# Down projection of a decoder layer: weight sums by adding DMAs, products reordered, a longer tile-by-tile end

## The chip, the cores and the metric

The kernel runs on one NeuronCore of a Trainium2 chip. Its time is in microseconds of the device, as the median of several runs. The profile is that of one more execution with the hardware profiler on. Times inside a profile are counted from the start of its span.

## The reference, cut to what matters

The kernel computes one whole decoder layer on a sequence of 1024 tokens with 1024 channels, in float32. The change touches only its last part, the down projection of the gated MLP, the norm of its output, and the residual sum:

```python
def conv_glu_ffn(h, w_up, conv_w, conv_b, w_down):
    u = causal_dwconv(h @ w_up, conv_w) + conv_b
    a, b = jnp.split(u, 2, axis=-1)
    return (jax.nn.silu(a) * b) @ w_down
...
        y = conv_glu_ffn(rmsnorm(h, g[4]), ffn_w_up[l], ffn_conv_w[l], ffn_conv_b[l], ffn_w_down[l])
        h = h + rmsnorm(y, g[5])
```

The hidden width is 2816, so the down projection is a product of 1024 x 2816 by 2816 x 1024.

## The kernel before

**The product.** The down projection is done by Strassen's scheme with seven products, M1 to M7, in place of eight block products. Rows (tokens), columns and the inner dimension are each halved. The 22 blocks of 128 hidden channels are taken in 11 pairs, the k pairs (`kp`): the first block of a pair belongs to the first half of the inner dimension, the second to the second. For each product and k pair, `down_operands` builds an operand tile `w` of the tag "w" (4 buffers), which holds a left block A (hidden channels by 512 tokens) and a right block B (hidden channels by 512 output columns), each in two float32r parts, high and low: ScalarE copies the high part, VectorE subtracts it from the float32 value to make the low part. `mm3` then multiplies high by high, high by low and low by high. A k pair is 12 matmuls of 128x128 by 128x512: four token tiles q, three each.

**The sums.** Most products need a sum or difference of two A blocks, of two B blocks or of both. A blocks are loaded once from `mid_d` in HBM, where the up projection left them, and stay in tiles named `ma`. B blocks are loaded anew for each use, from the weights, into tiles `rb` (tags "raw" and "braw", 2 buffers each, used in turn). A sum of A blocks is made by GpSimd (line 1299); one of B blocks by GpSimd as well, or by VectorE where the product also has a sum of A blocks (line 1301). Both go to tiles of the tag "sum" (`sM` in the profile). The split of a tile with two sums is `split` (lines 132 and 133); that of other tiles is lines 1308 to 1313.

**The order.** `todo` lists the steps (product, k pair) in order, M4, M3, M5, M2, M1, M6, M7, and `fetch(4)` keeps four operand tiles prepared or being prepared. A list scheduler of the framework then sets each engine's instruction order. The four accumulators of a product are PSUM banks; M6 adds onto the banks of M2 and M7 onto those of M1. When a token tile of a product is finished, `done` adds it from PSUM into the float32 tiles `yacc` (VectorE), and where a half row of the output is complete, `square` (ScalarE) sums its squares and `gained` (VectorE) multiplies it by the norm's gain. `final` makes the root factor, adds `yacc` times the factor to the residual `fin`, and stores the result. For token tiles 4 to 7 the finals are put off into a list `pend` and taken from it during M7, one at each odd k pair. The last four k pairs (`LAST`) of M7 are done token tile by token tile, with `final` behind each. The residual tiles `fin` have two buffers.

Of the kernel before, what the change touches and what calls it, by code (L numbers as in the profile page):

```python
# [7 lines left out]
F32 = mybir.dt.float32  # L8
F32R = mybir.dt.float32r
I32 = mybir.dt.int32  # L10
AF = mybir.ActivationFunctionType
ALU = mybir.AluOpType
# [4 lines left out]
P = 128  # L17
T = 1024
D = 1024
# [50 lines left out]
def hybrid_layer(  # L70
# [4 lines left out]
    nc = tc.nc  # L75
    act, dve, pe, sync = nc.scalar, nc.vector, nc.tensor, nc.sync

    def pool(name, bufs=1, side=None, space=None):
        kw = {} if space is DRAM else {"reuse_waits": "tile"}
        if side is not None:  # L80
            kw["side"] = side
        if space is not None:
            kw["space"] = space
        return tc.tile_pool(name=name, bufs=bufs, **kw)
# [16 lines left out]
    mid_d = dram.tile([NFF, P, T], F32, name="mid_d")  # L101

    const = ctx.enter_context(pool("const"))
    wpool = ctx.enter_context(pool("wpool"))
# [13 lines left out]
    def psum(tag, name):  # L118
        p, tags = psum_pool[0]
        return p.tile([P, 512], F32, tag=tag, name=name, bufs=tags[tag])  # L120
# [9 lines left out]
    def split(w, raw, gain=None):  # L130
        if gain is None:
            act.activation(w[:, 0], raw, AF.Copy)  # L132
            dve.tensor_tensor(w[:, 1], raw, w[:, 0], op=ALU.subtract)  # L133
        else:
            act.activation(w[:, 0], raw, AF.Identity, scale=gain)
            dve.scalar_tensor_tensor(out=w[:, 1], in0=raw, scalar=gain, in1=w[:, 0],
                                     op0=ALU.mult, op1=ALU.subtract)

    def raw_tile(shape, name):
        return wpool.tile(list(shape), F32, tag="raw", name=f"raw_{name}", bufs=2)  # L140
# [99 lines left out]
    HS = (slice(0, 512), slice(512, 1024))  # L240
# [299 lines left out]
    pend = []  # L540
# [487 lines left out]
    for t in range(NC):  # L1028
# [20 lines left out]
        r = rms_r(ss, 1, "r2")  # L1049
# [197 lines left out]
    for j in range(PLAIN, NFF):  # L1247
        if j + 1 < NFF:
# [7 lines left out]

    dr = ctx.enter_context(pool("dr", side="right"))
    dl = ctx.enter_context(pool("dl"))  # L1260
    g5 = row_gain(5, gbp)
    NP = NFF // 2
    yacc = [dl.tile([P, D], F32, name=f"yacc{t}") for t in range(NC)]
    ss5 = small(NC * 2, "ss5", bufs=1)
    LAST = 4

    PRODS = (("M4", ("22",), ("21", "11", -1)), ("M3", ("11",), ("12", "22", -1)),
             ("M5", ("11", "12", 1), ("22",)), ("M2", ("21", "22", 1), ("11",)),
             ("M1", ("11", "22", 1), ("11", "22", 1)), ("M6", ("21", "11", -1), ("11", "12", 1)),
             ("M7", ("12", "22", -1), ("21", "22", 1)))  # L1270
    res = {}

    def a_block(b, kp):

        if (b, kp) not in res:
            res[b, kp] = (dr if b == "22" and kp < 8 else dl).tile([P, 512], F32, name=f"ma{b}_{kp}")
            sync.dma_start(out=res[b, kp], in_=mid_d[2 * kp + int(b[1]) - 1][:, HS[int(b[0]) - 1]])
        return res[b, kp]

    n_step = [0]  # L1280

    def down_operands(m, kp):
        name, ab, bb = PRODS[m]
        p, tag = ((wpool, "raw"), (dr, "braw"))[n_step[0] % 2]
        n_step[0] += 1
        A_s = [a_block(b, kp) for b in ab[:2]]
        rb = p.tile([P, 2, 512], F32, tag=tag, name=f"rb{name}_{kp}", bufs=2)

        at = lambda b: w_down[2 * kp + int(b[0]) - 1][:, HS[int(b[1]) - 1]]
        bs = bb[:2]  # L1290
        for i, b in enumerate(bs):
            sync.dma_start(out=rb[:, i], in_=at(b))
        w = wpool.tile([P, 2, 2, 512], F32R, tag="w", name=f"w{name}_{kp}", bufs=4)
        sums = None
        if len(ab) == 3 or len(bb) == 3:
            sums = dr.tile([P, 2, 512], F32, tag="sum", name=f"s{name}_{kp}", bufs=2)
        alu = lambda s: ALU.add if s > 0 else ALU.subtract
        if len(ab) == 3:
            nc.gpsimd.tensor_tensor(sums[:, 0], A_s[0], A_s[1], op=alu(ab[2]))  # L1299
        if len(bb) == 3:  # L1300
            (dve if len(ab) == 3 else nc.gpsimd).tensor_tensor(sums[:, 1], rb[:, 0], rb[:, 1], op=alu(bb[2]))
        if len(ab) == 3 and len(bb) == 3:

            split(w, sums)
        else:
            for i, r in enumerate((sums[:, 0] if len(ab) == 3 else A_s[0], sums[:, 1] if len(bb) == 3 else rb[:, 0])):
                if name == "M2" and i == 1:
                    act.activation(w[:, 0, i], r, AF.Copy, scale=-1.0)
                    dve.scalar_tensor_tensor(out=w[:, 1, i], in0=r, scalar=-1.0, in1=w[:, 0, i],
                                             op0=ALU.mult, op1=ALU.subtract)  # L1310
                else:
                    act.activation(w[:, 0, i], r, AF.Copy)
                    dve.tensor_tensor(w[:, 1, i], r, w[:, 0, i], op=ALU.subtract)
        return w

    def square(t, n):
        jk = dl.tile([P, 512], F32, tag="junk", name="sqj", bufs=2)
        act.activation(jk, yacc[t][:, HS[n]], AF.Square, accum_out=ss5[:, 2 * t + n:2 * t + n + 1])

    def add_to(t, n, o, sign=1):  # L1320
        y = yacc[t][:, HS[n]]
        dve.tensor_tensor(y, y, o, op=ALU.add if sign > 0 else ALU.subtract)

    def gained(t, n):
        y = yacc[t][:, HS[n]]
        dve.tensor_tensor(y, y, g5[:, HS[n]], op=ALU.mult)

    def final(t, fin, first):

        r = sqrt_r(ss5_sum(t), 1, "r5")  # L1330
        for i, n in enumerate((first, 1 - first)):
            dve.scalar_tensor_tensor(out=fin[:, HS[n]], in0=yacc[t][:, HS[n]], scalar=r, in1=fin[:, HS[n]],
                                     op0=ALU.mult, op1=ALU.add)
            (sync, nc.scalar)[i].dma_start(out=out[t * P:(t + 1) * P, HS[n]], in_=fin[:, HS[n]])
# [3 lines left out]
        dve.tensor_tensor(s1, ss5[:, 2 * t:2 * t + 1], ss5[:, 2 * t + 1:2 * t + 2], op=ALU.add)  # L1338
        return s1

    def residual(t):
        fin = dl.tile([P, D], F32, tag="fin", name=f"fin{t}", bufs=2)
        sync.dma_start(out=fin, in_=h2_d[t])
        return fin

    def done(name, q, o):

        lo, hi = q, q + 4
        if name == "M4":
            act.activation(yacc[hi][:, HS[0]], o, AF.Copy)  # L1350
            act.activation(yacc[lo][:, HS[0]], o, AF.Copy)
        elif name == "M3":
            act.activation(yacc[lo][:, HS[1]], o, AF.Copy)
            act.activation(yacc[hi][:, HS[1]], o, AF.Copy)
        elif name == "M5":
            add_to(lo, 0, o, -1)
            add_to(lo, 1, o)
            square(lo, 1)
            gained(lo, 1)
        elif name == "M2":  # L1360
            add_to(hi, 0, o, -1)
            square(hi, 0)
            gained(hi, 0)
        elif name == "M1":
            add_to(hi, 1, o)
        elif name == "M6":
            add_to(hi, 1, o)
            square(hi, 1)
            gained(hi, 1)
            pend.append(lambda: final(hi, residual(hi), 0))  # L1370
        else:
            add_to(lo, 0, o)
            square(lo, 0)
            gained(lo, 0)
            final(lo, fins.pop(lo), 1)

    fins = {}
    todo = [(m, kp) for m in range(len(PRODS)) for kp in range(NP)]
    dops = {}

    def fetch(n):
        while todo and len(dops) < n:
            s = todo.pop(0)
            dops[s] = down_operands(*s)

    def step_mm(o, w, q, start, stop, onto):
        s = slice(q * P, (q + 1) * P)
        mm3(o, w[:, 0, 0, s], w[:, 1, 0, s], w[:, 0, 1], w[:, 1, 1], start, stop, onto)

    banks = [None, None]  # L1390
    for m, (name, _, _) in enumerate(PRODS):
        onto = name in ("M6", "M7")
        if not onto:
            banks[m % 2] = [psum("b", f"{name}_{q}") for q in range(4)]
        o = banks[m % 2]
        early = NP - LAST if name == "M7" else NP
        for kp in range(early):
            fetch(4)
            w = dops.pop((m, kp))
            for q in range(4):  # L1400
                step_mm(o[q], w, q, kp == 0 and not onto, kp == NP - 1, onto)
                if kp == NP - 1:
                    done(name, q, o[q])
            if pend and name == "M7" and kp % 2:
                pend.pop(0)()
    flush()
    fetch(LAST)
    for q in range(4):
        fins[q] = residual(q)
        for kp in range(NP - LAST, NP):  # L1410
            step_mm(banks[0][q], dops[len(PRODS) - 1, kp], q, False, kp == NP - 1, True)
        done("M7", q, banks[0][q])
    psum_es[0].close()


# [60 lines left out]
```

## Time and profile before

| | |
|---|---|
| Median of 3 runs | 1512.68 us (1509.54 to 1512.87) |
| The profiled execution | 1516.54 us, its span 1514.5 us |
| Mean granted TensorE clock | 0.984 of full speed |
| Busy share of the span | TensorE 95%, VectorE 78%, ScalarE 46%, GpSimd 20% |
| Down projection, first matmul to last | 1263.0 to 1497.2 us |

PE is TensorE's matmuls, PEld its weight loads, DVE is VectorE, ACT ScalarE, POOL GpSimd, SP the engine whose queue issues most DMAs; a q behind an engine is its instruction queue. `xcount` is the number of instructions in a row; a bracket behind a row tells how long the engine was idle before it and what ended that.

### The profile page before, as it was taken

What the parts mean: (1) busy time and instruction counts of PE and PEld (TensorE: products, weight loads), DVE (VectorE), ACT (ScalarE), POOL (GpSimd) and SP (SyncE); (2) the same over time, 40 slices, a digit from 0 to 9 for tenths busy, and PEclk for the clock granted to TensorE, in tenths of its full rate; (3) what the DMA queues carried; (4) which work ended last, traced back from release to release, by engine and by line L of the source; (5) the groups of instructions that cost most, each with busy time, mean ns of one, the idle gap of its engine ahead of it and who ended that gap; (6) DMA issues with size and microseconds to landing.
All of it is one profiled execution on the core that took longest, in us unless ns stands there. A gap on an engine that the chain in (4) does not pass through costs nothing.

```text
span 1514.5 us, 19535 instructions
## 1 busy us (share of the span) xinstructions
PE 1445.2 (95%) x7099; PEld 1189.5 (79%) x7099; DVE 1179.0 (78%) x1938; ACT 698.9 (46%) x1348; POOL 301.2 (20%) x195
## 2 busy tenths in 40 slices
PE   6999999999999899999999979999999999999984
PEld 6878888888897778788888858888888887887763
DVE  6799999983577777734555877888888888869996
ACT  6527455533565445433433534444444444554342
POOL 0000000000000000000001543333333334655651
PEclk9999999999999999999999989999999999999997
DMA  7523133339656765401423112222222227964545
GB/s 250 173 75 124 44 112 84 112 111 327 185 160 211 241 209 179 149 1 42 154 85 110 43 56 84 78 76 84 84 84 84 84 84 260 317 201 161 184 160 176
DMA packets 118560, 205.74 MB, mean 136 GB/s; under 512 B 17184, under 2 KB 58816, under 8 KB 118464
## 3 DMA queue, kind: packets, MB, share of 16 engines
q1 hardware_dynamic: 95488, 155.99, 33.2%
q10 hardware_dynamic: 22976, 48.51, 8.6%
q8 instruction: 56, 0.92, 0.3%
q14 instruction: 40, 0.33, 0.1%
HBM read 153.58 MB, written 50.87 MB: 135 GB/s over the span
## 4 chain that ended last, share of the span: by engine, by line
PE 70%; DVE 13%; DMA 8%; issue 4%; ACT 3%; POOL 1%; SPq 0%; DVEq 0%; ACTq 0%; POOLq 0%
PE st L236 8%; PE st L238 8%; PE st L237 8%; PE pj L238 6%; PE pj L236 6%; PE pj L237 6%; DVE wM L133 3%; PE M L237 2%; PE M L236 2%; PE M L238 2%; PE y L237 2%; PE y L238 2%; PE y L236 2%; PE sc L237 1%; PE sc L236 1%
## 5 line engine op out<-in xcount | busy, mean ns | idle before, releaser
L352 DVE SCALAR_TENSOR_TENSOR ca<-sg,par,ca 128x1023 f32<-128x1023 f32 (+18 forms) x120 | 150.3, 1268 | 1.1
L236 PE MATMUL pj<-xT,w_in 128*128 128x512 f32 x384 | 150.8, 393 | 0.1
L238 PE MATMUL pj<-xT,w_in 128*128 128x512 f32 x384 | 150.3, 391 | 0.5 <-DVE w_in L133 0.5
L237 PE MATMUL pj<-xT,w_in 128*128 128x512 f32 x384 | 149.9, 390 | 0.0
L1198 POOL TENSOR_TENSOR xr<-x,x 128x256 f32<-128x256 f32 x32 | 32.4, 1045 | 582.6 <-DVE hr L1106 565.4
L237 PE MATMUL M<-wM 128*128 128x512 f32 x308 | 124.9, 406 | 9.8 <-DVE wM L133 5.7
L1127 DVE SCALAR_TENSOR_TENSOR ua<-ua,par 128x1023 f32<-128x1023 f32 x88 | 117.0, 1329 | 11.3 <-ACT ua L1125 8.4
L236 PE MATMUL M<-wM 128*128 128x512 f32 x308 | 120.8, 397 | 2.2 <-ACT wM L132 2.2
L238 PE MATMUL M<-wM 128*128 128x512 f32 x308 | 121.6, 395 | 0.0
L236 PE MATMUL st<-xT,wst 128*128 128x512 f32 x304 | 118.7, 391 | 0.0
L238 PE MATMUL st<-xT,wst 128*128 128x512 f32 x304 | 118.4, 390 | 0.0
L237 PE MATMUL st<-xT,wst 128*128 128x512 f32 x304 | 118.2, 389 | 0.0
L1299 POOL TENSOR_TENSOR sM<-ma,ma 128x512 f32<-128x512 f32 x55 | 95.1, 1732 | 73.5 <-DVE wM L133 45.0
L236 PE MATMUL st<-x,wst 128*128 128x512 f32 x228 | 93.3, 409 | 9.6 <-ACT ua L1216 5.7
L238 PE MATMUL st<-x,wst 128*128 128x512 f32 x228 | 91.0, 399 | 0.0
L237 PE MATMUL st<-x,wst 128*128 128x512 f32 x228 | 90.9, 399 | 0.0
L1157 DVE TENSOR_TENSOR wst<-sums,wst 128x512 fp32r<-128x512 f32 x76 | 60.7, 819 | 35.0 <-ACT wst L1156 35.0
L1156 ACT ACTIVATE wst<-sums 128x512 fp32r<-128x512 f32 x76 | 43.8, 621 | 90.0 <-POOL sums L1151 90.0
L237 PEld LDWEIGHTS M<-wM 128*128 128x128 f32 x308 | 58.9, 191 | 33.0 <-DVE wM L133 15.3
L238 PEld LDWEIGHTS pj<-xT,w_in 128*128 128x128 f32 x384 | 72.1, 188 | 15.4 <-DVE w_in L133 0.8
L236 PEld LDWEIGHTS pj<-xT,w_in 128*128 128x128 f32 x384 | 72.0, 188 | 14.9 <-ACT w_in L132 0.3
L237 PEld LDWEIGHTS pj<-xT,w_in 128*128 128x128 f32 x384 | 72.2, 188 | 14.5
(380 smaller groups left out, 3782.6 us busy)
## 6 DMA issues: line engine op xcount, KB each, us to landing
rbM<-in_w_down SPq DMA_DIRECT2D x132, 256.0 KB, 3.5
raw_up<-in_w_up SPq DMA_DIRECT2D x44, 512.0 KB, 3.6
raw_in<-in_w_in SPq DMA_DIRECT2D x24, 512.0 KB, 3.7
mid_d<-ua ACTq DMA_DIRECT2D x22, 512.0 KB, 2.6
ma<-mid_d SPq DMA_DIRECT2D x44, 256.0 KB, 5.0
raw_kv<-in_w_kv SPq DMA_DIRECT2D x16, 512.0 KB, 4.2
h_d<-h ACTq DMA_DIRECT2D x16, 512.0 KB, 2.7
xr<-in_x ACTq DMA_DIRECT2D x8, 512.0 KB, 5.3
```

The costliest lines, as they stand in the source:

```text
L133: dve.tensor_tensor(w[:, 1], raw, w[:, 0], op=ALU.subtract)
L236: pe.matmul(o, lhsT=wh, rhs=xh, start=start, stop=False, skip_group_check=onto)
L237: pe.matmul(o, lhsT=wh, rhs=xl, start=False, stop=False, skip_group_check=onto)
L238: pe.matmul(o, lhsT=wl, rhs=xh, start=False, stop=stop, skip_group_check=onto)
L352: dve.scalar_tensor_tensor(out=ca[:, d:], in0=sg[:, :T - d], scalar=par[:, wb + 30 - d:wb + 31 - d], in1=ca[:, d:], op0=ALU.mult, op1=ALU.add)
L1127: dve.scalar_tensor_tensor(out=a[:, d:], in0=u[:, :T - d], scalar=fw(2 - d), in1=a[:, d:], op0=ALU.mult, op1=ALU.add)
L1156: act.activation(w[:, i, 0], op[s], AF.Copy)
L1157: dve.tensor_tensor(w[:, i, 1], op[s], w[:, i, 0], op=ALU.subtract)
L1198: nc.gpsimd.tensor_tensor(raw[n], X[n][0][:, :, s], X[n][1][:, :, s], op=ALU.add)
L1299: nc.gpsimd.tensor_tensor(sums[:, 0], A_s[0], A_s[1], op=alu(ab[2]))
```

## The change

B sums are no longer made by an engine: the first block is loaded by SP as before, and then a DMA issued from GpSimd's queue (`accum_op=ALU.add`) adds the second block to it in the buffer. To make all but one of the B combinations sums, the signs of some blocks are turned: A combinations are all differences now, made by VectorE into the `rb` tile, and only M1 has a difference of B blocks, by VectorE too. The tag "sum" is gone, and "braw" has 4 buffers, used for two steps of three.

The order of products is M4, M3, M2, M1, M6, M5, M7. Gain products and finals that follow M2, M6 and M5 are put into `pend`, from which one is taken at each odd k pair of any product. The blocks A21 lie in three tiles of four; when these are free, they hold the operands of three k pairs of M7 (5, 6, 7), which are prepared within the last steps of M5. The last six k pairs of M7 are done token tile by token tile, and all four residual tiles are loaded ahead of them, two into buffers of the tag "raw".

```diff
-    LAST = 4
-
-    PRODS = (("M4", ("22",), ("21", "11", -1)), ("M3", ("11",), ("12", "22", -1)),
-             ("M5", ("11", "12", 1), ("22",)), ("M2", ("21", "22", 1), ("11",)),
-             ("M1", ("11", "22", 1), ("11", "22", 1)), ("M6", ("21", "11", -1), ("11", "12", 1)),
-             ("M7", ("12", "22", -1), ("21", "22", 1)))
+    LAST = 6
+
+
+    PRODS = (("M4", 0, ("22",), ("21", "11")), ("M3", 1, ("11",), ("12", "22")),
+             ("M2", 0, ("22", "21"), ("11",)), ("M1", 1, ("11", "22"), ("11", "22")),
+             ("M6", 0, ("21", "11"), ("11", "12")), ("M5", 0, ("11", "12"), ("22",)),
+             ("M7", 1, ("12", "22"), ("21", "22")))
+    ENDP = len(PRODS) - 1
+
+    EXTRA = (5, 6, 7)
...
-            res[b, kp] = (dr if b == "22" and kp < 8 else dl).tile([P, 512], F32, name=f"ma{b}_{kp}")
-            sync.dma_start(out=res[b, kp], in_=mid_d[2 * kp + int(b[1]) - 1][:, HS[int(b[0]) - 1]])
+            if b == "21":
+                if kp % 4 == 0:
+                    g = dl.tile([P, 4, 512], F32, tag="a21", name=f"ma21_{kp}", bufs=3)
+                    for i in range(4):
+                        res[b, "t", kp + i] = g[:, i]
+                t = res[b, "t", kp]
+            else:
+                t = (dr if b == "22" and kp < 8 else dl).tile([P, 512], F32, name=f"ma{b}_{kp}")
+            res[b, kp] = t
+            sync.dma_start(out=t, in_=mid_d[2 * kp + int(b[1]) - 1][:, HS[int(b[0]) - 1]])
...
-        name, ab, bb = PRODS[m]
-        p, tag = ((wpool, "raw"), (dr, "braw"))[n_step[0] % 2]
+        name, _, ab, bb = PRODS[m]
+        p, tag, bufs = (wpool, "raw", 2) if n_step[0] % 3 == 0 else (dr, "braw", 4)
...
-        bs = bb[:2]
-        for i, b in enumerate(bs):
-            sync.dma_start(out=rb[:, i], in_=at(b))
-        w = wpool.tile([P, 2, 2, 512], F32R, tag="w", name=f"w{name}_{kp}", bufs=4)
-        sums = None
-        if len(ab) == 3 or len(bb) == 3:
-            sums = dr.tile([P, 2, 512], F32, tag="sum", name=f"s{name}_{kp}", bufs=2)
-        alu = lambda s: ALU.add if s > 0 else ALU.subtract
-        if len(ab) == 3:
-            nc.gpsimd.tensor_tensor(sums[:, 0], A_s[0], A_s[1], op=alu(ab[2]))
-        if len(bb) == 3:
-            (dve if len(ab) == 3 else nc.gpsimd).tensor_tensor(sums[:, 1], rb[:, 0], rb[:, 1], op=alu(bb[2]))
...
+        sync.dma_start(out=rb[:, 1], in_=at(bb[0]))
+        if name == "M1":
+            sync.dma_start(out=rb[:, 0], in_=at(bb[1]))
+            dve.tensor_tensor(rb[:, 1], rb[:, 1], rb[:, 0], op=ALU.subtract)
+        elif len(bb) == 2:
+            nc.gpsimd.dma_start(out=rb[:, 1], in_=at(bb[1]), accum_op=ALU.add)
+        if m == ENDP and kp in EXTRA:
+            w = dl.tile([P, 2, 2, 512], F32R, tag="a21", name=f"w{name}_{kp}", bufs=3)
         else:
...
+            w = wpool.tile([P, 2, 2, 512], F32R, tag="w", name=f"w{name}_{kp}", bufs=4)
+
+        if len(ab) == 2:
+            dve.tensor_tensor(rb[:, 0], A_s[0], A_s[1], op=ALU.subtract)
+            split(w, rb)
+        else:
+            for i, r in enumerate((A_s[0], rb[:, 1])):
+                act.activation(w[:, 0, i], r, AF.Copy)
+                dve.tensor_tensor(w[:, 1, i], r, w[:, 0, i], op=ALU.subtract)
...
-    def residual(t):
-        fin = dl.tile([P, D], F32, tag="fin", name=f"fin{t}", bufs=2)
+    def residual(t, last=False):
+        fin = raw_tile((P, D), f"fin{t}") if last else dl.tile([P, D], F32, tag="fin", name=f"fin{t}", bufs=2)
...
-            gained(hi, 0)
+            pend.append(lambda: gained(hi, 0))
...
-            gained(hi, 1)
-            pend.append(lambda: final(hi, residual(hi), 0))
+            pend.append(lambda: (gained(hi, 1), final(hi, residual(hi), 0)))
+        elif name == "M5":
+            add_to(lo, 0, o)
+            add_to(lo, 1, o, -1)
+            square(lo, 1)
+            pend.append(lambda: gained(lo, 1))
...
-    todo = [(m, kp) for m in range(len(PRODS)) for kp in range(NP)]
+    todo = [(m, kp) for m in range(ENDP) for kp in range(NP)]
+    for n, kp in enumerate(EXTRA):
+        todo.insert(len(todo) - 3 + n, (ENDP, kp))
+    todo += [(ENDP, kp) for kp in range(NP) if kp not in EXTRA]
...
-    def fetch(n):
-        while todo and len(dops) < n:
+    def fetch():
+        extra = lambda s: s[0] == ENDP and s[1] in EXTRA
+        while todo and (extra(todo[0]) or sum(not extra(s) for s in dops) < 4):
...
-            if pend and name == "M7" and kp % 2:
+            if pend and kp % 2 and kp < NP - 1:
                 pend.pop(0)()
     flush()
-    fetch(LAST)
+    fetch()
+    fins.update({q: residual(q, q > 1) for q in range(4)})
     for q in range(4):
-        fins[q] = residual(q)
```

## Rows read from the trace of the kernel before

**Rows 1.** The page, its first line.

```profile
span 1514.5 us, 19535 instructions
```

**Rows 2.** Stretches: length, busy us of PE, PEld, DVE, ACT, POOL; clock, DMA share, GB/s.

```profile
1263.02:1279.00 15.98, 12.82 (x52) 9.18 (x51) 14.78 (x15) 7.73 (x12) 10.30 (x6) 1.00 0.84 304
1279.00:1297.41 18.41, 18.41 (x82) 15.20 (x81) 18.26 (x17) 9.08 (x16) 12.78 (x9) 1.00 0.97 345
1297.41:1327.33 29.92, 29.92 (x133) 24.77 (x132) 23.89 (x24) 17.66 (x33) 19.30 (x13) 1.00 0.90 293
...
1357.25:1388.24 30.99, 30.22 (x134) 24.70 (x132) 30.69 (x34) 15.10 (x27) 15.63 (x11) 1.00 0.46 151
1388.24:1419.97 31.73, 31.34 (x133) 24.39 (x132) 31.48 (x28) 12.97 (x18) 18.39 (x10) 1.00 0.52 167
1419.97:1452.96 32.99, 32.60 (x134) 23.92 (x132) 32.68 (x27) 11.66 (x12) 19.17 (x11) 1.00 0.54 173
1452.96:1497.30 44.34, 36.99 (x133) 26.98 (x131) 41.37 (x68) 17.33 (x31) 16.53 (x9) 0.88 0.48 163
1497.30:1514.50 17.20, 0.00 (x0) 0.00 (x0) 8.31 (x26) 1.31 (x4) 0.00 (x0) 0.61 0.57 183
```

**Rows 3.** Timeline of TensorE: first matmul, one k pair in M4, last matmul.

```profile
1263.02 0.39 PE L236 MATMUL M<-wM 128*128 128x512 f32 x1
...
1286.53 0.39 PE L236 MATMUL M<-wM 128*128 128x512 f32 x1
...
1289.25 0.39 PE L236 MATMUL M<-wM 128*128 128x512 f32 x1
...
1496.84 0.39 PE L238 MATMUL M<-wM 128*128 128x512 f32 x1
```

**Rows 4.** Tile wM (ns min/median/max), then the timeline of VectorE and GpSimd.

```profile
L133 DVE TENSOR_TENSOR wM<-sM,wM x33: 1211/1226/2321, 1383.7 to 1489.2; 128x1024 fp32r<-128x1024 f32 x33
...
1356.67 1.88 DVE L1322 TENSOR_TENSOR yacc<-yacc,M 128x512 f32<-128x512 f32 x3
...
1420.24 0.69 DVE L1301 TENSOR_TENSOR sM<-rbM 128x512 f32<-128x512 f32 x1
1420.29 1.80 POOL L1299 TENSOR_TENSOR sM<-ma,ma 128x512 f32<-128x512 f32 x1 [1.16 <-DVE wM L133]
1420.85 2.32 DVE L133 TENSOR_TENSOR wM<-sM,wM 128x1024 fp32r<-128x1024 f32 x1
1423.20 0.69 DVE L1301 TENSOR_TENSOR sM<-rbM 128x512 f32<-128x512 f32 x1
```

**Rows 5.** Timeline of SP, GpSimd and TensorE at the start of M4.

```profile
1257.87 0.91 SPq L1292 DMA_DIRECT2D rbM<-in_w_down  x2
...
1262.88 2.13 POOL L1301 TENSOR_TENSOR sM<-rbM 128x512 f32<-128x512 f32 x1 [14.49 <-DMA ma<-mid_d]
...
1267.83 0.50 PE L237 MATMUL M<-wM 128*128 128x512 f32 x1 [0.91 <-DVE wM L1313]
```

**Rows 6.** DMA issues from 1255 to 1300 us, median us to landing.

```profile
rbM<-in_w_down SPq DMA_DIRECT2D x34, 256.0 KB, 5.1
```

**Rows 7.** Timeline of TensorE in M7, behind a gap.

```profile
1484.51 1.22 PE L236 MATMUL M<-wM 128*128 128x512 f32 x2 [2.19 <-ACT wM L132]
1485.53 0.63 PE L237 MATMUL M<-wM 128*128 128x512 f32 x1
1485.95 0.63 PE L238 MATMUL M<-wM 128*128 128x512 f32 x1
```

**Rows 8.** DMA issues from 1495 us on, and the timeline of VectorE.

```profile
fin<-h_d SPq DMA_DIRECT2D x2, 512.0 KB, 4.0
...
1498.98 0.68 DVE L1322 TENSOR_TENSOR yacc<-yacc,M 128x512 f32<-128x512 f32 x1
...
1502.86 0.16 DVE L217 SCALAR_TENSOR_TENSOR r_y<-r_u,r_y 128x1 f32<-128x1 f32 x1
...
1509.96 1.41 DVE L1332 SCALAR_TENSOR_TENSOR fin<-yacc,r_y,fin 128x512 f32<-128x512 f32 x2 [3.40 <-DMA fin<-h_d]
```

More of the change, by code (lines that the diff above doesn't have):

```diff
@@ L1282, in down_operands @@
     def down_operands(m, kp):
-        name, ab, bb = PRODS[m]
-        p, tag = ((wpool, "raw"), (dr, "braw"))[n_step[0] % 2]
+        name, _, ab, bb = PRODS[m]
+        p, tag, bufs = (wpool, "raw", 2) if n_step[0] % 3 == 0 else (dr, "braw", 4)
         n_step[0] += 1
-        A_s = [a_block(b, kp) for b in ab[:2]]
-        rb = p.tile([P, 2, 512], F32, tag=tag, name=f"rb{name}_{kp}", bufs=2)
+        A_s = [a_block(b, kp) for b in ab]
+        rb = p.tile([P, 2, 512], F32, tag=tag, name=f"rb{name}_{kp}", bufs=bufs)
@@ L1300, in down_operands @@
-        if len(bb) == 3:
-            (dve if len(ab) == 3 else nc.gpsimd).tensor_tensor(sums[:, 1], rb[:, 0], rb[:, 1], op=alu(bb[2]))
-        if len(ab) == 3 and len(bb) == 3:
-            split(w, sums)
-        else:
[L1306 to L1313, printed above, removed]
+        sync.dma_start(out=rb[:, 1], in_=at(bb[0]))
@@ L1354, in done @@
             act.activation(yacc[hi][:, HS[1]], o, AF.Copy)
[L1355 to L1359, printed above, removed]
         elif name == "M2":
@@ L1390, in hybrid_layer @@
     banks = [None, None]
-    for m, (name, _, _) in enumerate(PRODS):
+    for m, (name, bset, _, _) in enumerate(PRODS):
         onto = name in ("M6", "M7")
         if not onto:
-            banks[m % 2] = [psum("b", f"{name}_{q}") for q in range(4)]
-        o = banks[m % 2]
-        early = NP - LAST if name == "M7" else NP
+            banks[bset] = [psum("b", f"{name}_{q}") for q in range(4)]
+        o = banks[bset]
+        early = NP - LAST if m == ENDP else NP
         for kp in range(early):
-            fetch(4)
+            fetch()
             w = dops.pop((m, kp))
@@ L1403, in hybrid_layer @@
                     done(name, q, o[q])
-            if pend and name == "M7" and kp % 2:
+            if pend and kp % 2 and kp < NP - 1:
                 pend.pop(0)()
     flush()
-    fetch(LAST)
+    fetch()
+    fins.update({q: residual(q, q > 1) for q in range(4)})
     for q in range(4):
-        fins[q] = residual(q)
         for kp in range(NP - LAST, NP):
-            step_mm(banks[0][q], dops[len(PRODS) - 1, kp], q, False, kp == NP - 1, True)
-        done("M7", q, banks[0][q])
+            step_mm(banks[1][q], dops[ENDP, kp], q, False, kp == NP - 1, True)
+        done("M7", q, banks[1][q])
     psum_es[0].close()
```

## The prediction

> **What bounds the kernel now.** I read the profile in this order: the page for the span, the table of stretches cut at the first matmul of each of the seven products, the timeline of TensorE, and then VectorE and GpSimd inside the stretches that came out long. The span is 1514.5 us [rows 1]; the profiled execution took 1516.54 us, 2.0 us more than its span and 3.9 us more than the median of the three runs. I work out a change against the span and take it off the median.
>
> Twelve matmuls make one k pair of one product, and from 1286.53 to 1289.25 they take 2.72 us [rows 3]. The 77 k pairs so need 209.4 us; from the first matmul at 1263.02 to the end of the last at 1497.23 [rows 3] they take 234.2 us. About 24.7 us is therefore TensorE standing still or running at a lower clock. Each stretch of [rows 2] holds some 132 matmuls, which need 29.9 us. M4 takes two of its rows, 34.4 us, so it loses 4.5; M3 loses nothing; M1 loses 1.8, M6 3.1 and M7 14.4; M2 loses 1.1.
>
> What M1, M6 and M7 wait for is seen in [rows 4]. The VectorE subtraction that makes the low part of a 128x1024 operand takes 1.21 us at its quickest and 2.32 us at its slowest, and each slow one lies beside a GpSimd tensor operation (1420.29 beside 1420.85). One step costs VectorE 2.96 us there (1420.24 to 1423.20 in two B sums), over the 2.72 us of TensorE: VectorE, held up by GpSimd, is the bound, and the final sums of token tiles 4 to 7, which this kernel puts into M7, have no slack to fall into. M7 also loses clock: the matmuls after the gap at 1484.51 follow each other at 0.43 us instead of 0.227 [rows 7], the lower of the two levels (1.2 GHz), and the granted share of M7's stretch is 0.88 [rows 2].
>
> After the last matmul 17.3 us go by [rows 2]. Two residual loads of 4.0 us each [rows 8] stand in that time, one behind the other, because a load waits until the previous output has left one of two `fin` buffers.
>
> **What goes away on VectorE.** With no GpSimd tensor operation left, I price the VectorE operations at their quick durations. Back to back, 128x512 ones start 0.60 us apart (three in 1.88 us) [rows 4], and the wide low part then costs 1.14. A step of M4 or M3 costs VectorE 1.2 us, of M2, M6, M5 or M7 0.60 + 1.14 = 1.74, of M1 2.34. All are under 2.72. ScalarE's work per step is unchanged. That the stalls of M2, M1, M6 and M7 (20.4 us) vanish follows, if the adding DMAs bring their sums in time and the moved work finds room; those are the next three parts. The products' order itself changes the number of neither matmuls nor loads.
>
> **The adding DMAs.** 44 loads of 256 KB (11 each in M4, M3, M6, M7) become loads that add into a buffer already loaded. The trace has none of these. In M4's second half the DMA engines were 0.97 busy at 345 GB/s [rows 2], so one plain 256 KB load is worth 262144 / 345000 x 0.97 = 0.74 us of all sixteen. An adding one costs at least one load, since it brings the same bytes; taken as a load, a read of the destination and a write apart, three. I take two (the nearest row is the plain load, and the one thing that must be added is the old value), and keep one and three. M4 and M3 are the hard place: per step one A block, one plain load, one adding load. From 1256, with the first and fourth step's weights preloaded in the `raw` buffers and the gain row in front, that is 64, 84 or 104 load times: 47, 62 or 77 us. Add 7 us for the last landing, the split and its matmuls, and M3 can end at 1310, 1325 or 1340. TensorE alone would end it at 1263.0 + 59.8 = 1323 plus what the start costs, so at two loads the DMAs just do not bind; at three they cost 10 us. In M6 and M7 there is no A block to load, and six buffered steps cover even four load times (2.96 us) a step for the most part. Latency is covered from then on: a buffer is free again six steps (16.3 us) before its next use is due. On the GpSimd queue each adding DMA waits for the plain load before it, and only other adding DMAs stand behind it.
>
> The Trainium skill, DMA: Bandwidth & Descriptors, section Rules for kernel authors, says that an accumulating DMA reads its destination and writes it later. No row here shows it; by it the price would be nearer two loads than one.
>
> **The start.** Step 0 keeps its time: its weights land from 1242 on and its A block decides. Step 1 does not. Its weights are issued at 1257.87 and GpSimd takes them up at 1262.88 [rows 5], 5.0 us later, the median landing there being 5.1 [rows 6]. Before, the low part then reached TensorE at 1267.83 [rows 5]. Now the second weight block is only asked for at 1262.9; with another 5.1 us it is there at 1268.0, and after a ScalarE copy, VectorE's part (behind the convolution of the last up-projection pair) and semaphores TensorE goes on at about 1271 instead of 1265.7: 5.5 us. A gap that long may cost clock as in M7, where a stretch at 0.43 us [rows 7] cost about 3 us; I add 1.5, so 7 us where M4 lost 4.5. Bounds: 3 us (landing as quick as 3 us, no clock lost) and 14 (10 us for the add, and the clock).
>
> **The moved work.** `final` of tiles 4 to 7 goes from M7 to M5, with its gain products, and three steps of M7 are prepared during M5. Two steps of M5 cost VectorE 3.48, one deferred entry 0.60 + 1.9 (two `fin` products, 1.41 [rows 8], and five small operations at about 0.1): 5.98 us against 5.44 of TensorE. Four entries leave VectorE 2.2 us behind, M6's four adds 1.4, the three extra splits 5.2: 8.8. An operand may be begun three steps (8.2 us) before its use and needs about 2.8 itself, so 5.4 are covered: 3 us of stall, nothing if the final sums give way, 9 if the cover is gone. M5 also takes PSUM banks that M6 has just filled; the four adds must be read out within one step: 0.5 us, between 0 and 2.
>
> **The tail.** Six k pairs tile by tile are 18 matmuls, 4.1 us a tile, more than VectorE's 3.1 for a finished tile, so only the last tile's chain is left behind TensorE; and with four residual buffers filled ahead, both 4 us loads are hidden by M7's last 16 us. What stays: from the last add to the last factor 4.0 us (1498.98 to 1503.02, with another tile's work between; without it not under 3), and from the last `fin` product to the end 1514.5 - 1509.96 = 4.5 [rows 8]. That is 8.5 us for 17.3, a gain of 8.8 (8 to 9.8).
>
> **Sum.** 24.7 of stalls go, 7 + 3 + 0.5 come back: 14.2. With 8.8 from the tail, 23.0 us. Span 1491.5, profiled execution 1493.5, median 1512.7 - 23.0 = 1490 us.
>
> **Rivals.**
> *The adding DMA costs three loads.* The share of 0.97 in M4 and 0.90 in M3 [rows 2] speaks for it; that later products use about half speaks against its reaching further. M3 ends 10 us later and a little more is lost in M6 and M7: 1502.
> *VectorE stays the bound in M5,* as it was in M7: the final sums wait in its queue for residual loads and ScalarE's root, and each odd step stalls as in M7 (14.4 us for a stretch). Against it: 0.98 us of slack a step, where M7 had none. 1490 + 11 = 1501.
> *GpSimd's issuing of the adding DMAs holds VectorE up* as its tensor operations did, so the slow form stays. If each of the 44 holds VectorE 1.1 us (2.32 - 1.21) [rows 4], M4 and M3 hide it (1.2 + 1.1), M6 and M7 come to 2.84 a step and M5's backlog grows by three: about 5 us, 1495. The Trainium skill, SBUF — State Buffer, section SBUF: two separate sides, states that VectorE in a two-port mode keeps GpSimd from writing the descriptors of a DMA; its section Who interferes with whom infers that tensor_tensor, by its read side alone, does not. The trace agrees that two tensor operations exclude each other and cannot show the descriptors.
> *Slower:* the adding DMA costs four loads or more in M4 and M3. Then these need 124 load times, 92 us, M3 ends at 1355, 25 us late, M6 and M7 lose some 5 more: 1520. It decides from about 3.8 loads on, where the 23 us are used up. Nothing in the trace excludes it; that bytes read and written should count four times speaks against it.
>
> **Chances.** My forecast 0.68 (1480 to 1498), three loads 0.09, M5 0.06, the lock 0.04, between 3.6 and 4 loads (no difference) 0.03, slower 0.10. Measurement tells 0.3% (4.5 us) from no change: faster 0.87, same 0.03, slower 0.10. Low end: 3 us at the start, nothing else, tail 9.8: 1481, and the runs spread 3 us, so 1480. High end: a start of 14 with M5 at 9, or three loads with some of either: 1506.
>
> **What would show it.** No GpSimd tensor operation after 1262; VectorE's wide low part near 1.22 us throughout. One gap of TensorE in step 1 of M4, then 2.72 us a step; DMA share under 0.95 in M3 (if the share is 1 and steps take 3 us or more, the adding DMA was mis-sized; its landing time says by how much). Gaps, if any, late in M5. Granted clock 1.00 from M3 on. No wait for a residual load at the end, and 8 to 9 us after the last matmul. A time over 1500 would mean that the DMA price or VectorE's load in M5 was wrong.

## The result, and the profile after

The changed kernel takes 1504.07 us (median; 1498.25 to 1507.02) where the kernel before, run beside it, took 1512.87: the ratio is 0.9934, with a 95% interval of 0.9915 to 0.9954. It is faster, as forecast, but by 9 us (10 by the ratio) in place of 23.

The page's first line answers to [rows 1]; the profiled execution, 1507.02 us, is again the slowest of its set.

```profile
span 1505.2 us, 19483 instructions
```

The table of stretches is cut as [rows 2] were, one row for each product in the new order M4, M3, M2, M1, M6, M5, M7, and one for the tail. Its columns are those of [rows 2]; the DMA share adds up the times of the packets, so it can pass 1.

```profile
1261.60:1300.00 38.40, 32.16 (x134) 26.10 (x133) 21.35 (x29) 16.59 (x26) 10.97 (x13) 0.91 0.96 271
1300.00:1334.30 34.30, 31.24 (x133) 24.50 (x132) 18.79 (x28) 18.60 (x33) 5.45 (x7) 1.00 1.08 330
1334.30:1364.30 30.00, 30.00 (x134) 24.82 (x133) 23.56 (x28) 14.15 (x17) 0.00 (x0) 1.00 0.69 243
1364.30:1394.20 29.90, 29.90 (x134) 24.75 (x133) 28.87 (x38) 14.07 (x19) 4.32 (x5) 1.00 0.67 168
1394.20:1424.10 29.90, 29.90 (x134) 24.75 (x133) 24.42 (x29) 12.40 (x13) 5.20 (x6) 1.00 0.72 166
1424.10:1455.90 31.80, 30.62 (x133) 24.59 (x132) 27.87 (x54) 16.47 (x23) 4.68 (x6) 1.00 0.77 201
1455.90:1495.83 39.93, 33.47 (x133) 25.28 (x132) 30.00 (x53) 13.04 (x24) 4.86 (x6) 0.96 0.60 163
1495.83:1505.23 9.40, 0.00 (x1) 0.00 (x0) 5.08 (x13) 1.02 (x3) 0.00 (x0) 0.72 0.30 112
```

A product needs 29.9 us. What a row has above that is stall or lower clock: M4 8.5, M3 4.4 (4.5 when cut at its first matmul, as in the next table), M2, M1 and M6 nothing, M5 1.9, M7 9.8 (its row also holds 0.16 us in which the last matmul drains). Together that is 24.6 us, as much as before: the old stalls are gone and as many new ones have come. What was gained is the tail, 9.4 us for 17.2. The first matmul also comes 1.4 us earlier, but the change hasn't done that: in the part before, which it doesn't touch, TensorE is 1.8 us ahead already at 630 us.

### The profile page after: what moved, and what is told of

The parts are those of the page before. It is cut to its first block, busy times and chain, and to the rows that moved or that the text cites. A ratio compares the mean times of both kernels' runs of the same rounds, so it can differ in the third digit from the quotient of the medians.

```text
span 1505.2 us, 19483 instructions
## 1 busy us (share of the span) xinstructions
PE 1440.2 (96%) x7099; PEld 1190.2 (79%) x7099; DVE 1137.0 (76%) x1949; ACT 695.3 (46%) x1326; POOL 207.9 (14%) x162
## 3 DMA queue, kind: packets, MB, share of 16 engines
q0 software_dynamic: 6336, 11.54, 4.5%
## 4 chain that ended last, share of the span: by engine, by line
PE 47%; DMA 7%; DVE 5%; issue 2%; ACT 2%; POOL 1%; SPq 0%; DVEq 0%; ACTq 0%; POOLq 0%
PE st L236 8%; PE st L238 8%; PE st L237 8%; DMA rbM<-in_w_down 4%; PE M L236 3%; PE M L237 2%; PE M L238 2%; PE y L237 2%; PE y L238 2%; PE y L236 2%; PE sc L236 2%; PE sc L237 2%; PE sc L238 2%; PE wo L238 1%; PE wo L237 1%
## 5 line engine op out<-in xcount | busy, mean ns | idle before, releaser
L132 ACT ACTIVATE wM<-rbM 128x1024 fp32r<-128x1024 f32 x55 | 57.4, 1060 | 65.4 <-PE M L238 36.3
```

## The experiments

One table for all runs. The stalls are read from each run's own profile as above; the ratios are to the kernel before, run on the same chip, whose median was 1512.87 to 1515.19 us. The first matmul of the down projection falls anywhere from 1257.2 to 1267.7 us in these profiles, though no edit touches what comes ahead of it. So single medians carry some us of that, and the stalls tell causes apart better. They have a spread of their own, since each comes from one execution: in the six runs that leave M4 and M3 as the change has them (the change, 3, 5, 7, 8, 9), M4's stalls are 7.9 to 9.2 us and M3's 3.6 to 5.3, and run 2, which leaves M5 and M7 as they are, loses 9.4 there for the change's 11.7. The change's own profile is of the slowest of its executions.

| Run | Median us | Ratio, 95% | M4 | M3 | M5 + M7 | Tail |
|---|---|---|---|---|---|---|
| the change | 1504.07 | 0.9934 [0.9915, 0.9954] | 8.5 | 4.5 | 11.7 | 9.4 |
| 1 plain loads for adding DMAs | 1494.69 | 0.9885 [0.9866, 0.9903] | 6.9 | 0 | 5.5 | 9.4 |
| 2 VectorE sums in M4, M3 | 1496.11 | 0.9874 [0.9854, 0.9893] | 6.4 | 0 | 9.4 | 9.6 |
| 3 M5's A blocks held back | 1501.79 | 0.9940 [0.9922, 0.9958] | 9.0 | 5.3 | 8.9 | 9.4 |
| 4 no adding DMA | 1495.26 | 0.9879 [0.9861, 0.9897] | 4.9 | 0 | 8.6 | 9.7 |
| 5 stores from the accumulator | 1500.31 | 0.9917 [0.9900, 0.9934] | 9.1 | 3.6 | 6.6 | 9.4 |
| 6 = 2 + 5 | 1494.84 | 0.9879 [0.9856, 0.9901] | 4.9 | 0 | 8.2 | 9.6 |
| 7 M5's sums spread over M7 | 1503.30 | 0.9941 [0.9922, 0.9960] | 8.0 | 4.6 | 7.1 | 9.3 |
| 8 tail's part undone | 1502.81 | 0.9931 [0.9908, 0.9954] | 9.2 | 4.0 | 4.0 | 13.9 |
| 9 no early steps, residuals ahead | 1500.36 | 0.9898 [0.9871, 0.9924] | 7.9 | 3.9 | 6.9 | 10.0 |
| 10 = 2 + 9 | 1489.76 | 0.9835 [0.9812, 0.9859] | 4.9 | 0 | 2.5 | 10.2 |
| 11 = 2 + 5 + 9 | 1486.70 | 0.9813 [0.9789, 0.9837] | 4.9 | 0 | 0.4 | 10.2 |
| 12 = 4 + 5 + 9 | 1493.44 | 0.9856 [0.9831, 0.9882] | 4.9 | 0 | 0.5 | 12.2 |

### 1. What the adding itself costs

```diff
-            nc.gpsimd.dma_start(out=rb[:, 1], in_=at(bb[1]), accum_op=ALU.add)
+            nc.gpsimd.dma_start(out=rb[:, 1], in_=at(bb[1]))
```

> The 44 adding DMAs become plain loads of the same bytes from the same GpSimd queue, at the same place and with the same waits (the second weight block overwrites the first, so the sums are left out). This separates what an adding DMA costs the DMA engines from what its place in the chain costs (a second load that is asked for only when the first has landed). Theory A (the engines' time: 160 ns a packet against 80): M3's stall falls from 4.5 us to under 1, M4's from 8.5 to about 6, M5's and M7's together from 11.7 to under 9, time 1497 or less. Rival B (the chain of two landings): M3 keeps 3 us, M4 7 and more, time 1501 or more.

The run leaves the sums out: the second block overwrites the first. Here is the page's part on DMA queues (packets, MB, share of 16 engines), the changed kernel's GpSimd queue first, with its issues (count, size, median us to landing):

```profile
q0 software_dynamic: 6336, 11.54, 4.5%
...
rbM<-in_w_down POOLq DMA_DIRECT2D x44, 256.0 KB, 6.7
```

and the same lines of this run:

```profile
q0 software_dynamic: 3520, 11.54, 2.2%
...
rbM<-in_w_down POOLq DMA_DIRECT2D x44, 256.0 KB, 4.9
```

An adding DMA takes 4.5% of 1505.2 us over 44, 1.54 us of all sixteen engines; a plain one 2.2% of 1492.9 over 44, 0.75. The price is two loads. Without it M3 stalls no more and M5 and M7 lose 6 us less: 7 us of time by the ratios and 9 by the medians hang on the adding alone, at the same place in the same queue with the same waits. The chain of two landings by itself doesn't make M3 stall, so rival B falls, and the rest came as theory A said, but that M4 keeps 6.9 us where it said 6; 5.0 of these stand in its first gap (6.2 with the adding).

How M3 comes to stall shows if its third step is followed from SP's issue of the first block, over the issue of the second, to ScalarE's split and the first matmul. The changed kernel (timeline of SP, GpSimd, ScalarE, TensorE):

```profile
1287.53 0.41 SPq L1303 DMA_DIRECT2D rbM<-in_w_down  x1
...
1296.54 0.86 POOL L1308 DMA_DIRECT2D rbM<-in_w_down  x1 [1.83 <-DMA rbM<-in_w_down]
...
1304.45 0.63 ACT L1319 ACTIVATE wM<-rbM 128x512 fp32r<-128x512 f32 x1 [2.54 <-DMA rbM<-in_w_down]
...
1305.40 0.39 PE L236 MATMUL M<-wM 128*128 128x512 f32 x1
```

and this run:

```profile
1284.27 0.37 SPq L1303 DMA_DIRECT2D rbM<-in_w_down  x1
...
1291.88 0.54 POOL L1308 DMA_DIRECT2D rbM<-in_w_down  x1 [1.33 <-DVE wM L1320]
...
1297.76 0.63 ACT L1319 ACTIVATE wM<-rbM 128x512 fp32r<-128x512 f32 x1 [0.98 <-DMA rbM<-in_w_down]
...
1303.81 0.39 PE L236 MATMUL M<-wM 128*128 128x512 f32 x1
```

From issue to split is 16.9 us in the one and 13.5 in the other; the mean of M3's eleven steps is 16.5 and 13.9, and a buffer is free only when VectorE has made the low part from it, some 1.5 us after that. Six buffers are worth six steps, 16.3 us. Over that, each round is late; under it, the split lies 6 us ahead of its matmul. Full DMA engines alone don't make a stall: in this run M3 goes through without a gap at a share of 1.05, to which loads that run ahead belong (SP has issued 44 A blocks up to its end). Its row, with the columns of [rows 2]:

```profile
1298.37:1328.29 29.92, 29.92 (x134) 24.77 (x132) 20.25 (x29) 17.56 (x32) 2.69 (x5) 1.00 1.05 388
```

### 2. VectorE makes the sums of M4 and M3

```diff
-        if name == "M1":
+        if name in ("M1", "M4", "M3"):
             sync.dma_start(out=rb[:, 0], in_=at(bb[1]))
-            dve.tensor_tensor(rb[:, 1], rb[:, 1], rb[:, 0], op=ALU.subtract)
+            dve.tensor_tensor(rb[:, 1], rb[:, 1], rb[:, 0], op=ALU.subtract if name == "M1" else ALU.add)
```

> The weight sums of M4 and M3 are made by VectorE again, from two plain loads, while M6 and M7 keep their adding DMAs. Theory A (the adding DMAs, at about two loads each, crowd the DMA engines in M4 and M3): the gap of M4's first step pair shrinks from 6.4 us to under 3, and M3's 4.5 us of stall shrink to under 2; with the clock that the gap cost, the time falls by about 5 us against the changed kernel, to some 1499. Rival B (the A blocks that later products ask for early are what crowds M3, and M4's gap is the landing of a plain load behind the queue's head): M3 keeps 3 us or more, and the time falls by at most 2 us. Rival C (VectorE, given 22 more sums, becomes the bound in M4 and M3 at 0.60 + 1.2 us a step): stalls there grow and the time rises; 1.8 us a step against 2.72 speaks against it. M7's 9.8 us of stall should stay under all three.

M3's row, cut as above:

```profile
1299.91:1329.83 29.92, 29.92 (x133) 24.77 (x132) 22.21 (x34) 16.21 (x29) 0.00 (x0) 1.00 0.84 278
```

M3 runs without a gap at a DMA share of 0.84, where it was 1.08, and VectorE is busy 22 of its 30 us. The gap of M4's first two steps is gone (0.4 us for 6.4), but two later steps lose 2.3 and 3.4 us. A and not B or C; the time falls by 8 us, more than the 5 expected. What M4 keeps here and in runs 4, 6 and 10 to 12, 4.9 to 6.4 us, is what it lost before the change (4.5) or a little more.

### 3. Loads that run ahead

```diff
+            if name == "M1":
+                held[kp] = dl.tile([P, 512], F32, name=f"ma12_{kp}")
+                dve.tensor_copy(out=held[kp][:, :1], in_=rb[:, 1, :1])
```

with `held[kp]` as M5's block, so that its load waits for M1's weights.

> The A blocks that M5 alone reads are not loaded before M1's weights of the same k pair have landed, where the changed kernel asks for them during M3 and M2. Theory A (these loads, run ahead, take the DMA engines that M3's adding DMAs need): M3's 4.5 us of stall fall under 2, time down by 2 to 4 us. Rival B (M3's own loads, with adding DMAs at two loads each, fill the engines by themselves): the stall stays at 3.5 or more and the time does not move.

M3 stalls 5.3 us and not less, though SP issues 33 A blocks up to its end and not 41. Rival B, as far as this run goes: M5's A blocks aren't what M3's weights wait for. The other loads that run ahead, those of M2, were left as they are.

### 4. No adding DMA

The edit is that of 2 for M6 and M7 too.

> No adding DMA at all: the weight sums of M4, M3, M6 and M7 are made by VectorE from two plain loads, and GpSimd does nothing here. This separates the change's two parts, no GpSimd tensor operations (kept) and adding DMAs (undone). Theory A (the gain came from freeing VectorE of GpSimd, and the adding DMAs only cost): time equal to the run with VectorE's sums in M4 and M3 alone or a little under it, 1496 to 1500; VectorE then has 0.60 + 0.60 + 1.14 = 2.34 us of work a step in M6 and M7, under 2.72. Rival B (VectorE needs the adding DMAs' relief in M6, M5 and M7, where final sums and extra splits are due too: a further 0.6 us for each of 22 steps, 13 us against some 10 us of slack there): new stalls of 3 us or more in M5 or M7, and 1502 or more.

1495.26 us, the same as 2 within the intervals. So adding DMAs cost more than VectorE's sums in the two products in which A blocks and weights are both loaded (M4, M3); in M6 and M7 they save VectorE about as much as they take. M5 and M7 still lose 8.6 us with no adding DMA there. That doesn't clear the adding of a part in their 11.7: run 1, which has neither its price nor VectorE's sums, loses 5.5.

### 5 and 6. Residual loads that wait for stores

```diff
-            dve.scalar_tensor_tensor(out=fin[:, HS[n]], in0=yacc[t][:, HS[n]], scalar=r, in1=fin[:, HS[n]], op0=ALU.mult, op1=ALU.add)
-            (sync, nc.scalar)[i].dma_start(out=out[t * P:(t + 1) * P, HS[n]], in_=fin[:, HS[n]])
+            y = yacc[t][:, HS[n]]
+            dve.scalar_tensor_tensor(out=y, in0=y, scalar=r, in1=fin[:, HS[n]], op0=ALU.mult, op1=ALU.add)
+            (sync, nc.scalar)[i].dma_start(out=out[t * P:(t + 1) * P, HS[n]], in_=y)
```

> A final sum writes its result over its own accumulator and stores from there, so that a residual buffer is free as soon as VectorE has read it, and the next residual load no longer waits for an output to leave. Theory A (a residual load that waits at the head of SP's queue for two stores holds back the weight loads of M7 behind it): M7's 9.8 us of stall fall under 4, M5's 1.9 under 1, and the time falls by 6 to 8 us, to some 1497. Rival B (M7 is late because its adding DMAs take 160 ns a packet and land late): M7's stall stays at 8 us or more and the time does not move. Rival C (VectorE's work for the final sums stands in M7's way): likewise no change, and VectorE shows no idle time in the first four steps of M7.

> Both edits: VectorE makes the weight sums of M4 and M3, and the final sums are stored from their accumulators. If the two causes are separate (the adding DMAs in M4 and M3; the residual loads on SP's queue in M5 and M7), the gains add up: 5 + 7 us, some 1492. If one of them only moves a stall to a later product, the gain is that of the better edit alone, 1497 to 1499.

In the changed kernel the steps from the second to the fourth of M7 are late like this (timeline of SP, GpSimd, ScalarE, VectorE, TensorE):

```profile
1442.44 0.33 SPq L1303 DMA_DIRECT2D rbM<-in_w_down  x1
1449.01 0.33 SPq L1350 DMA_DIRECT2D fin<-h_d  x1
1449.43 0.89 SPq L1303 DMA_DIRECT2D rbM<-in_w_down  x2
...
1451.29 0.86 POOL L1308 DMA_DIRECT2D rbM<-in_w_down  x1 [8.79 <-DMA rbM<-in_w_down]
1455.53 1.75 POOL L1308 DMA_DIRECT2D rbM<-in_w_down  x2 [3.38 <-DVE r_u L216]
...
1458.85 1.06 ACT L132 ACTIVATE wM<-rbM 128x1024 fp32r<-128x1024 f32 x1 [3.16 <-DMA rbM<-in_w_down]
1463.25 1.06 ACT L132 ACTIVATE wM<-rbM 128x1024 fp32r<-128x1024 f32 x1 [3.34 <-DMA rbM<-in_w_down]
...
1465.48 4.87 DVE L1329 TENSOR_TENSOR yacc<-yacc,M 128x512 f32<-128x512 f32 x8
...
1471.07 1.99 ACT L132 ACTIVATE wM<-rbM 128x1024 fp32r<-128x1024 f32 x2
...
1472.16 1.60 PE L236 MATMUL M<-wM 128*128 128x512 f32 x4 [3.71 <-ACT wM L132]
```

The second step's weights are issued at 1442.44 and land 8.3 us later; GpSimd, which waits for them, adds to them at 1451.29, that lands 7.4 us later, and ScalarE splits at 1458.85: two long landings, one behind the other. SP then issues nothing for 6 us, since the residual load at its head waits for a `fin` buffer; behind it, at 1449.43, come the weights of the third and fourth step. GpSimd adds to them at 1455.53 and 1456.20, and ScalarE waits for the third step's at 1463.25. Then M5's eight sums fill VectorE for 4.9 us, ScalarE squares what they leave, and the fourth step's split, whose weights have landed at 1465.2, comes at 1471.07. In run 5 M7's stall falls from 9.8 to 2.4 us, but M5's rises from 1.9 to 4.2, and the time falls by about 4 us (3 by the ratios, whose intervals overlap), not 6 to 8. Together with 2 it adds nothing that can be measured (1494.84 to 1496.11). Theory A names a part, not the whole.

### 7. M5's sums spread over M7

```diff
-            add_to(lo, 0, o)
-            add_to(lo, 1, o, -1)
-            square(lo, 1)
-            pend.append(lambda: gained(lo, 1))
+            pend.append(lambda: (add_to(lo, 0, o), add_to(lo, 1, o, -1), square(lo, 1), gained(lo, 1)))
```

and one entry is taken after each of M7's early steps.

> M5's accumulator sums (eight on VectorE) and four squares (ScalarE) no longer stand together between M5 and M7; each token tile's share is done after one of M7's first four steps, behind the operand that the step prepares. Theory A (this block of some 4.8 us on VectorE, and ScalarE waiting in it, holds back the splits of M7's steps): the 5.1 us stall between the third and the fourth step of M7 falls under 2, with its clock M7 goes from 9.8 to 6 or less, time down by 3 to 5 us. Rival B (the operands are late because of SP's queue and landings alone): the stall stays, and VectorE shows idle time in its place.

The 5.1 us stall falls to 0.6, but small ones (0.3 to 1.2 us) now stand at each of the first seven steps, and the time is the same, though this profile has 7.1 us of stall in M5 and M7 for 11.7. Neither theory as put: the block of sums does hold the splits back, but moving it doesn't gain time. That VectorE is left with as much to do in the same stretch would explain this; no run shows it.

### 8 and 9. The tail's part undone, and half of it

Run 8 has `LAST = 4`, `EXTRA = ()` and one residual load between each two tiles; run 9 has `LAST = 4` and `EXTRA = ()` alone, and its edit is shown.

```diff
-    LAST = 6
+    LAST = 4
...
-    EXTRA = (5, 6, 7)
+    EXTRA = ()
```

> The tail's part of the change undone: the last four k pairs, not six, go token tile by token tile, no steps of M7 are prepared ahead, and the residual loads of tiles 0 to 3 come one by one between the tiles from two buffers. Theory A (the tail was priced rightly): time behind the last matmul goes from 9.4 back to about 17 us, some 8 us more; M5 and M7 lose less, since three splits (5 us of VectorE) are not due early: 0 to 4 us back. Time 1508 to 1512. Rival B (the tail would be short without it): under 1505.

> One half of the tail's part alone: the four residual loads stay ahead of the tile-by-tile matmuls, but those are the last four k pairs and no step of M7 is prepared ahead. Theory A (in M5 and M7 VectorE has no room for three more splits, and the four loads ahead are what shortens the tail): stalls of M5 and M7 fall from 11.7 to about 4 us, as they did with the whole tail part undone; the tail is 10 to 11.5 us (twelve matmuls a tile are 2.72 us against VectorE's 3.1), time 1497 to 1499. Rival B (the six k pairs are what shortens the tail): the tail stays at 13 us or more, time 1501 or more. Rival C (the stalls come from the residual loads ahead): stalls 8 us or more.

With all of it undone the tail is 13.9 us, not 17, and M5 and M7 lose 7.7 us less: the time doesn't change (0.9931 to 0.9934). The tail's part took 4.5 us from the end and put about as much into M5 and M7. Run 9 shows that the four loads ahead make the tail short (10.0 us) and that six k pairs tile by tile, for which three operands must be ready early, make 0.6 us of it (M5 and M7 lose 6.9 us with the four loads ahead and 4.0 without, not much over the spread of such readings). Its M7 still loses 6.8 us, 5.4 of them at one step with the lower clock behind it (granted 0.50, 1.2 GHz, from 1479 to 1485), where ScalarE waits 3.57 us for weights that stand behind a residual load. So its time fell less than expected.

### 10 to 12. The causes taken away together

> The same, and the weight sums of M4 and M3 on VectorE. If the two causes (adding DMAs in M4 and M3; three early splits in M5 and M7) are separate, their gains of 8 and 6 us add up: 1490. If the second only showed because of the first, 1494 to 1496.

> The same, and the final sums stored from their accumulators, so that a residual load waits for VectorE alone. With no early splits the residual loads at the head of SP's queue are the stall left in M7 (2.5 us at one step with the tail undone): 1 to 3 us less than without this edit, 1487 to 1490. Rival: nothing, since SP's queue runs far enough ahead.

> The same without any adding DMA: all weight sums on VectorE. If M6's and M7's adding DMAs relieve VectorE where the final sums are due, this is 2 us or more slower than with them; if they only take DMA time and hold back SP's queue, equal or up to 3 us faster (1486 to 1489).

Run 10: 1489.76, as expected from two separate causes; by the ratios run 2's edit is worth 9.1 us, run 9's 5.4, and both together 15.0. Run 11: 1486.70, the fastest of all; its rows for M4, M3, M5 and M7, and the tail:

```profile
1259.26:1294.00 34.74, 31.22 (x132) 24.57 (x133) 31.85 (x47) 19.37 (x32) 0.00 (x0) 1.00 0.98 346
1294.00:1324.00 30.00, 30.00 (x134) 24.82 (x133) 22.38 (x34) 16.30 (x29) 0.00 (x0) 1.00 0.90 300
...
1413.70:1443.80 30.10, 30.10 (x134) 24.74 (x133) 29.31 (x56) 15.61 (x22) 4.67 (x6) 1.00 0.80 239
1443.80:1474.10 30.30, 30.30 (x133) 24.48 (x131) 26.38 (x43) 13.74 (x25) 4.82 (x6) 1.00 0.68 171
1474.10:1484.31 10.21, 0.00 (x1) 0.00 (x0) 6.54 (x18) 1.31 (x4) 0.00 (x0) 0.61 0.42 154
```

M5 and M7 run through at full clock. Here, with no early steps, run 5's edit is worth 2.1 us of stall (2.4 at one step of M7 in run 10, 0.2 here). Run 12 shows what the adding DMAs of M6 and M7 are good for: without them VectorE is still at earlier tiles' `final` when M7 ends, and the tail grows by 2.0 us; the other 4.7 us of difference don't come from it, as far as the profiles tell: in them the first matmul stands at 1267.7 against 1259.3, and 6 us of this are there already at 634 us, in a part that no edit touches.

## Why the prediction was off, point by point

**GpSimd and VectorE: right, but not for all of the 20.4 us.** The stalls of M2, M1 and M6, 6.0 us, are gone. The wide low part, 1211/1226/2321 ns in [rows 4], is now even (min/median/max of tile `wM`):

```profile
L133 DVE TENSOR_TENSOR wM<-rbM,wM x55: 1217/1222/1233, 1331.6 to 1480.5; 128x1024 fp32r<-128x1024 f32 x55
```

Its maximum of 1233 ns, though 16 of these 55 run while GpSimd issues an adding DMA, rules out the rival in which their issue holds VectorE up. That is what the Trainium skill, SBUF — State Buffer, section Who interferes with whom, infers of `tensor_tensor` and descriptors.

The other 14.4 us, M7's, the prediction put down to the same cause from a row of M6. In M7 itself the low part was mostly quick before the change; what was slow there beside a GpSimd operation were for the most part small ones, 1.2 us in place of 0.2 (timeline of VectorE and GpSimd before; then SP's own waits from 1450 to 1497 us):

```profile
1463.27 1.22 DVE L133 TENSOR_TENSOR wM<-sM,wM 128x1024 fp32r<-128x1024 f32 x1
...
1473.23 3.88 POOL L1299 TENSOR_TENSOR sM<-ma,ma 128x512 f32<-128x512 f32 x2 [3.01 <-DVE wM L133]
...
1475.90 1.23 DVE L216 SCALAR_TENSOR_TENSOR r_u<-r_y,r_a 128x1 f32<-128x1 f32 x1
...
1486.93 0.21 DVE L216 SCALAR_TENSOR_TENSOR r_u<-r_y,r_a 128x1 f32<-128x1 f32 x1
...
SPq L1343 <- DMA out<-fin: 12.2, 4, 4.4
```

Each operation's time less the quickest of its kind adds up to some 8 us of VectorE in M7, an estimate, so the hold-up is a part of its 14.4. What the rest was isn't shown; SP's residual loads (L1343) waited 12.2 us for stores there already, a wait that the prediction's account of M7 doesn't have.

**The start: right in mechanism, 1.5 us short.** Forecast: GpSimd at 1262.9, the sum at 1268.0, TensorE at 1271, with some clock lost. In the profile (GpSimd, ScalarE, TensorE):

```profile
1263.12 0.86 POOL L1308 DMA_DIRECT2D rbM<-in_w_down  x1 [7.59 <-DMA rbM<-in_w_down]
...
1270.02 0.63 ACT L1319 ACTIVATE wM<-rbM 128x512 fp32r<-128x512 f32 x1 [4.75 <-DMA rbM<-in_w_down]
...
1270.70 1.65 PE L236 MATMUL M<-wM 128*128 128x512 f32 x3 [6.24 <-ACT wM L1319]
```

M4 lost 8.5 us where 7 were forecast: 6.24 of gap for 5.5 (its own figures, 1271 less 1265.7, give 5.3) and 2.3 of lower clock for 1.5. In runs 2, 4, 6 and 10 to 12 this gap goes with the adding DMA, but M4 then loses 4.9 to 6.4 us in its first steps, so that the adding and its chain cost it some 2 to 4 us more than VectorE's sums do.

**The adding DMA's price: right. "Latency is covered from then on": wrong, 4.5 us.** Two loads were taken, 1.54 against 0.75 us measured. The Trainium skill, DMA: Bandwidth & Descriptors, section Rules for kernel authors, has the destination read and later written, and the prediction took that for nearer two loads than one; the measured price agrees. But the prediction used the price for a sum over M4 and M3 as a whole, in which "the DMAs just do not bind", and put the turn of a buffer at 16.3 us without adding up what fills it: two landings, one behind the other, each long while the engines are full (medians over M4 and M3: 7.1 us for the plain load, 6.9 for the adding one, against 5.1 in [rows 6]), and a split. At the step shown above it comes to 16.9. The sum was short as well: from 1255 to the end of M3 SP issued 41 A blocks, where 22 were counted, 25 first weight blocks and two residual tiles of double size. Run 3 says that M5's A blocks among them weren't decisive, run 1 that the adding was. Whether the adding binds by the engines' time or by its longer landing in the chain, no run tells apart: the share was 1.08, but 1.05 without a stall in run 1, and the turn 16.9 us.

**The moved work: the step that failed most, 11.7 us for 3.5.** "An operand may be begun three steps (8.2 us) before its use and needs about 2.8 itself, so 5.4 are covered" counted VectorE and ScalarE alone. In the changed kernel VectorE isn't the bound there all the time, it waits: from 1424 to 1472 VectorE waits 8.2 us for ScalarE, and ScalarE 12.3 us for weights. The three extra operands each take a turn of a weight buffer, their first blocks issued by 1435; M7's own first steps come behind them, in two landings each, and the weights of its third and fourth step behind a residual load on SP's queue. The upper bound of 9, "if the cover is gone", was the nearer figure. Without the early steps and with VectorE's sums in M4 and M3 the loss is 2.5 us (run 10), with free residual loads 0.4 (run 11). The adding's own time is in it too: without it, and with the early steps, the loss is 5.5 (run 1). How the 11.7 divide among early steps, adding and residual loads stays open: taken away singly they give back 6.2 us (adding, run 1), 5.1 (residual loads that wait for stores, run 5) and 4.8 (early steps, run 9), together more than there is. The rival "VectorE stays the bound in M5" named the final sums' wait for residual loads, but on VectorE's queue; the wait was on SP's, with weights behind it. In run 4, with VectorE's work at its largest, M7's row shows it busy 34.5 of 38.6 us, so there that rival comes nearest.

**The tail: right in size, wrong in worth.** 8.5 us forecast, 9.4 found: each tile's chain takes 4.6 us, not 3.1, since VectorE also waits for ScalarE's square (0.85 us) and root (0.17), so the last add comes 1.6 us after TensorE. But its two halves have different prices: the residual loads ahead give nearly all of it (13.9 to 10.0, run 8 to run 9), and the longer tile-by-tile part cost some 7 us in M5 and M7 (9.4 to 2.5, run 2 to run 10) for 0.6 in the tail.

**The sum.** 24.7 of stalls went; 8.5 + 4.5 + 11.7 came back where 7 + 0 + 3.5 were forecast, 14.2 us more than the sum had; the tail gave 7.9 us for 8.8. The "slower" rival (four loads) and that of three loads fall with the price of two.

## What to carry to other kernels

Price a DMA in a chain twice: its share of the engines over the stretch, and the turn of its buffer, from issue over every landing in the chain to the last reader, against the number of buffers times the step; a second transfer that waits for the first may fit the one and not the other. Work that is moved ahead needs a turn of every buffer on its way, not only engine time, and a load that waits for a buffer at the head of an in-order queue stops all loads behind it (here for 6 us). When the total of stalls stays the same, cut both traces by stage before looking for one cause: here two of the change's parts each gave back what another had won.

## What the runs showed that was not expected

An adding DMA of 256 KB costs GpSimd 0.86 us to issue, a plain one from the same queue 0.54, and in 6336 packets where the plain ones are 3520; its median landing is 6.7 us against 4.9. Time that the change's own tail saved was almost wholly due to when the residual tiles are asked for: moving four 512 KB loads ahead takes the tail from 13.9 to 10.0 us without any other edit.
